# K's low part on 128 rows, the sink by a matmul of ones, and narrower masks in two attention stages

## The chip, the cores and the metric

One core of one Trainium2 chip runs a whole program of two transformer blocks on 1024 tokens. The time is device microseconds of one execution; the kernel before took 3023.18 us as the median of 3 runs (3018.93 to 3025.36). In the names below PE is TensorE (PEld its weight loads), DVE VectorE, ACT ScalarE, POOL GpSimd, SP the engine that issues most DMAs.

## The reference

Only two functions of it are touched by the change. In the first block, sliding-window attention with a sink, 8 heads of 64 over 2 heads of K and V, in 8 blocks of 128 queries:

```python
def gqa_sink_attend(qb, keys, vals, bias, sink_g):
    s = jnp.einsum('bqkgd,bskd->bkgqs', qb, keys) * (DH_A ** -0.5) + bias
    s_sink = jnp.broadcast_to(sink_g[None, :, :, None, None], (b, KV_A, G_A, q, 1))
    p = jax.nn.softmax(jnp.concatenate([s, s_sink], axis=-1), axis=-1)[..., :-1]
    return jnp.einsum('bkgqs,bskd->bqkgd', p, vals)

# for block i: keys are 256 context tokens and up to 384 tokens around the block,
# valid = abs(tq - ts) <= 128 and 0 <= ts < 1024
```

In the second block, chunk-band attention, 8 heads of 64: each chunk of 64 queries sees its own chunk and the 8 before it, with a bias by distance:

```python
s = jnp.einsum('bqhd,bkhd->bhqk', qc, kc) * scale + bias
s = jnp.where(valid, s, -jnp.inf)
p = jax.nn.softmax(s, axis=-1)
out = jnp.einsum('bhqk,bkhd->bqhd', p, vc)
```

## The kernel before

Precise products are made of fp32r parts: a number is a high part (rounded) and a low part (the rest). A head has only 64 features, so Q's high part lies on 64 partitions and its low part on the other 64, and K's high part stands on both halves. One matmul of 128 rows then gives (Q high + Q low) times K high. A second matmul on 64 rows gives Q high times K low.

**Window stage** (`phase_window`, L457, about 194 to 424 us). For each of the 8 query blocks, `win_scores` is called for two groups of four heads. For a head it takes a scores buffer of two PSUM banks (`big`, two rotate; L41 is the matmul helper `mm`) and writes: the sink's column, by an fp32 matmul of the identity with a column of `sink` (L354 loads it, on all partitions); the mask, by an fp32r matmul of the identity `identr` with 384 columns (256 in blocks 0 and 7), of which the middle 128 are zeros; then the band of 384 (or 256) keys and the 256 context keys, high part on 128 rows, low part on 64 rows. VectorE takes the maximum (L510), ScalarE the exponential with its sum (L512), VectorE scales (L517). `win_pv` of the block before transposes the probabilities (L44), copies them (L532 on ACT, L534 on DVE) and multiplies by V into 64 columns of the array (`t<-PT,Va`, tile 128*64). Between blocks pieces of another product are called in, `mods` (`t<-wmod,ct`, tile 128*32), whose weights SP streams from DRAM. The constants are prepared at the end of `phase_win` by GpSimd (L353 to L356); GpSimd's next work is the low part of h (L62).

The lines of `win_scores` that matter:

```python
self.mm(ps[:, 768:769], self.ident, sink[:, h:h + 1], True, True)
self.mm(band, identr, mask[:, mo:mo + bw], True, False)
self.mm(band, q, ks[:, g, kb], False, False)
self.mm(ctx, q, ks[:, g, 0:256], True, False)
self.mm(band, q[r], kl[r, g, kb], False, True)
self.mm(ctx, q[r], kl[r, g, 0:256], False, True)
```

`kl` stands on both halves of the partitions already (`put_k`, L399).

**Band stage** (`phase2_mix`, about 1921 to 2085 us). For 4 pairs of heads, 8 query blocks and the 2 heads of a pair, `band_scores` writes the bias by two matmuls with the reversal `Jr` (high `bh` and low `bl`), K's high part `bks` on 128 rows for the far keys (up to 384) and the near ones (up to 256), in the blocks with five key tiles a far mask `mfr` of 256 columns by the identity, and K's low part `bkl` on 64 rows. Maximum (L1550), exponential (L1552), reciprocal and scaling follow, and `band_pv` transposes (L44), copies (L1572) and multiplies by V (tile 128*64). `band_pair` (L1499) makes the parts of a pair: of the low part (L1515) only the 64 partitions that are used, on VectorE for the first two pairs and GpSimd for the others. Some matmuls of the gated branch lie between.

The order on each engine is not written out here: the framework's planner orders the instructions by its own estimates, and may put matmuls of one head behind those of other work.

Of the kernel before, what the change touches and what calls it, by code (L numbers as in the profile page):

```python
# [6 lines left out]
F32 = mybir.dt.float32  # L7
F32R = mybir.dt.float32r
# [25 lines left out]
class Build:  # L34
# [11 lines left out]
    def warm(self, src, n):  # L46
        """keeps the tensor engine's clock up while the first operands of a phase are made"""
        ps = self.pa()
        for _ in range(n):
            self.mm(ps, src[:, :128], src[:, :512], True, True)  # L50
# [13 lines left out]
    def rsqrt(self, ss, scale, eps=EPS, way="act"):  # L64
        """1 / sqrt(ss * scale + eps) for a small tile"""
# [8 lines left out]
    def rsqrt_bits(self, v, eng):  # L74
        """1 / sqrt(v) by Newton's steps from the exponent's half"""
# [56 lines left out]
    def mod_slab(self, pool, s, ps, bufs):  # L132
        """rows 32g (and 32g + 1: ctx) of ps = silu(c) @ w_mod[:, s * 2048 + g * 512 ...]; yields between loads"""
# [24 lines left out]
    def mod_cols(self):  # L158
        """slab 0 as columns: shift, scale of the first norm"""
# [10 lines left out]
    def norm1(self, xp):  # L170
        """x, ctx -> h^T (hi, lo), two tiles of tokens between yields"""
# [74 lines left out]
    def load_w(self, pool, src, n, ks=8, kb=2, tag="w", rawbufs=3, bufs=5, rk=None):  # L246
        """DRAM [ks*128, n] -> list over k of (hi [128, n], lo [128, n])"""
# [14 lines left out]
    def acc3(self, ps, L, R, k, last):  # L262
        """ps += (Lhi+Llo)^T (Rhi+Rlo) without lo*lo"""
        self.mm(ps, L[0], R[0], k == 0, False)
        self.mm(ps, L[0], R[1], False, False)
        self.mm(ps, L[1], R[0], False, last)

    def phase_win(self):
# [15 lines left out]
        mask = vap.tile([128, 384], F32R, name="mask")  # L284
        sink = vap.tile([128, 8], F32, name="sink")
        self.win_consts = identr, mask, sink
# [5 lines left out]
        with self.pool("t0") as st:  # L292
            mraw = st.tile([128, 384], F32, name="mraw")
# [59 lines left out]
            nc.gpsimd.dma_start(mraw, I["maskA"])  # L353
            nc.gpsimd.dma_start(sink, I["sink"].to_broadcast([128, 8]))  # L354
            nc.gpsimd.tensor_copy(identr, self.ident)
            nc.gpsimd.tensor_copy(mask, mraw)  # L356

# [4 lines left out]
        # ka  # L362
# [13 lines left out]
        # cq  # L376
# [22 lines left out]
    def put_k(self, s, x):  # L399
        """rotated keys [128 (two heads), s] -> hi and lo, each on both halves of the partitions"""  # L400
# [9 lines left out]
    def put_q(self, m, s, x):  # L410
        """rotated queries of heads 2m, 2m + 1 -> hi on one half of the partitions, lo on the other"""
# [7 lines left out]
    def gemm_fm(self, ps, w, c0, act, half_outer=False):  # L419
        """ps [128, 1024] = W[:, c0:c0+128]^T act"""  # L420
# [36 lines left out]
    def phase_window(self, mods):  # L457
        nc, tc, I = self.nc, self.tc, self.I
        with self.pool("wa", "right") as wa:
            qs, ks, kl = self.qs, self.ks, self.kl  # L460
            identr, mask, sink = self.win_consts
            pend = None
            for b in range(8):
                u = self.win_block(wa, b)
                self.win_scores(wa, u, 0, qs, ks, kl, identr, mask, sink)
                if pend:
                    self.win_pv(wa, pend)
                self.win_scores(wa, u, 1, qs, ks, kl, identr, mask, sink)
# [21 lines left out]
    def win_scores(self, wa, u, g, qs, ks, kl, identr, mask, sink):  # L490
# [5 lines left out]
        mo = 0 if b else 128  # L496
        P = []
        for h in range(g * 4, g * 4 + 4):
            r = slice((h % 2) * 64, (h % 2) * 64 + 64)
# [4 lines left out]
            self.mm(ps[:, 768:769], self.ident, sink[:, h:h + 1], True, True)  # L504
            self.mm(band, identr, mask[:, mo:mo + bw], True, False)
            self.mm(band, q, ks[:, g, kb], False, False)
            self.mm(ctx, q, ks[:, g, 0:256], True, False)
            self.mm(band, q[r], kl[r, g, kb], False, True)
            self.mm(ctx, q[r], kl[r, g, 0:256], False, True)
            nc.vector.reduce_max(nm[:, h:h + 1], ps[:, c0:769], axis=AX.X, negate=True)  # L510
            p = wa.tile([128, 642], F32, name="P", bufs=12)
            nc.scalar.activation(p[:, :W + 1], ps[:, c0:769], AF.Exp, bias=nm[:, h:h + 1], accum_out=sm[:, h:h + 1])  # L512
# [93 lines left out]
    def mla_init_k(self, s, w):  # L606
        """the rows of K that all pairs share: rotated keys, the maximum's -1 and zeros between"""
# [43 lines left out]
    def mla_row_max(self, s):  # L651
        """rows of Q: the largest score of every query, from the leading parts"""
# [25 lines left out]
    def mla_early(self):  # L678
        """the first pair of heads: leading parts and largest scores"""
# [175 lines left out]
    def logits(self, wo, h2, t, wr):  # L855
        """the router's scores of the tokens of the tiles h2, the first of them tile t"""
# [33 lines left out]
    def router_softmax(self, g0, g1):  # L890
        """softmax over the experts for groups g0..g1 of two tiles (tile 2g + i at [:, i, g])"""
# [183 lines left out]
    def norm2_tile(self, xp, x, nf, nm, t):  # L1075
        """h^T of a tile of tokens: the final norm of block 1 and the first of block 2 at once"""
# [233 lines left out]
    def gdn_local(self, gp, c):  # L1310
        """k^T, q^T, P^T and U of a chunk, kept in DRAM, with U's diagonal blocks of 32 apart"""
# [30 lines left out]
    def gdn_invert(self, gp):  # L1342
        """(I - U)^-1 of all 128 diagonal blocks of 32, one to a partition, by back substitution"""
# [17 lines left out]
    def gdn_solve(self, gp, c):  # L1361
        """R = (I - U)^-1 of a chunk from its diagonal blocks; yields between stages"""
# [111 lines left out]
    def band_prep(self, bp):  # L1474
# [15 lines left out]
        m = bp.tile([128, 256], F32, name="mfar")  # L1490
        nc.vector.memset(m, 0.0)
        nc.vector.memset(m[64:128, 0:64], -1e30)
        self.mfar = bp.tile([128, 256], F32R, name="mfr")
        nc.vector.tensor_copy(self.mfar, m)

    def band_pair(self, bp, m):
# [7 lines left out]
        for e in range(2):  # L1504
# [10 lines left out]
            eng.tensor_sub(kl[r, e], T[1, e][r], ks[r, e].bitcast(F32))  # L1515
# [5 lines left out]
    def band_scores(self, bp, m, b, pre):  # L1521
# [9 lines left out]
        for e in range(2):  # L1531
            r = slice(e * 64, e * 64 + 64)
# [10 lines left out]
            if nk == 5:  # L1543
                self.mm(ps[:, c0:c0 + 256], self.idr, self.mfar, False, False)
            if far:
                self.mm(pf, q[r], kl[r, e, kf], False, True)
            self.mm(pn, q[r], kl[r, e, kn], False, True)
# [69 lines left out]
    def branch_a(self):  # L1617
        """the gated branch a of the first 256 features, while the bands leave room on the tensor engine"""
# [247 lines left out]
def prepare(inputs):  # L1866
# [6 lines left out]
    A = {}  # L1873
# [35 lines left out]
    z = np.zeros((128, 128), f32)  # L1909
# [56 lines left out]
```

## Time and profile before

| | us |
|---|---|
| median of 3 runs | 3023.18 |
| span of the profiled execution | 3023.2 |
| window stage, first block's third head to the end | 224 to 424 |
| band stage | 1921 to 2085 |

| engine | busy us | share of the span |
|---|---|---|
| TensorE matmul | 2843.3 | 94% |
| TensorE weight load | 2196.4 | 73% |
| VectorE | 1785.1 | 59% |
| ScalarE | 1132.4 | 37% |
| GpSimd | 643.4 | 21% |

The busy time of TensorE is the union of matmuls whose recorded durations overlap in a stream. For the price of one matmul one reads the distance between the starts of neighbours. The granted clock is given as a share: 1.00 is 2.4 GHz, 0.50 is 1.2 GHz.

### The profile page before, as it was taken

The numbers are of one execution on the slowest core, as the hardware profiler recorded it, in microseconds if no ns is written. First come the engines' busy times: TensorE is split into PE (matmuls) and PEld (weight loads), VectorE is DVE, ScalarE is ACT, GpSimd is POOL, SyncE is SP. The second block draws the span as 40 slices with busy tenths as digits, with TensorE's granted clock in tenths as the row PEclk, the third lists the DMA queues.
The fourth block names the chain that finished last, engine by engine and source line by source line (L and its number), as shares of the span: only waits on it lengthen the run. The fifth ranks groups of instructions, "written<-read, shape, count | busy, mean of one in ns | idle before, by whom it ended". The sixth has DMA issues, their size and how long they took to land. (4 is left out here: it accounts for less than half of the span.)

```text
span 3023.2 us, 36522 instructions
## 1 busy us (share of the span) xinstructions
PE 2843.3 (94%) x14196; PEld 2196.4 (73%) x14196; DVE 1785.1 (59%) x2675; ACT 1132.4 (37%) x1756; POOL 643.4 (21%) x622
## 2 busy tenths in 40 slices
PE   6999999999994999789999899999999999999997
PEld 3885556445673777578889788777898888888886
DVE  3654457888567999766436333375655445445445
ACT  4443445334423676553321223454133222222223
POOL 1000013333433888522121332130000000000000
PEclk8998999999996999999999999999999999999999
DMA  6123200000437999822453545212522111111111
GB/s 217 41 69 105 91 29 8 1 1 22 130 128 253 353 372 371 259 64 84 143 183 113 192 140 147 83 37 74 177 85 84 49 52 53 42 49 49 42 35 56
DMA packets 179965, 338.81 MB, mean 112 GB/s; under 512 B 17545, under 2 KB 104457, under 8 KB 177489
## 3 DMA queue, kind: packets, MB, share of 16 engines
q1 hardware_dynamic: 161408, 270.13, 26.9%
q0 software_dynamic: 18384, 66.35, 6.9%
q8 instruction: 112, 1.84, 0.3%
q14 instruction: 61, 0.49, 0.0%
HBM read 282.95 MB, written 53.49 MB: 111 GB/s over the span
## 5 line engine op out<-in xcount | busy, mean ns | idle before, releaser
L62 DVE TENSOR_TENSOR mlo<-mraw,mhi 128x2048 fp32r<-128x2048 f32 x63 | 220.1, 3520 | 9.6 <-ACT mhi L59 9.5
L41 PE MATMUL big<-hhi,wuhi 128*128 128x512 f32 x672 | 214.8, 396 | 0.0
L41 PE MATMUL big<-hhi,wulo 128*128 128x512 f32 x672 | 213.3, 396 | 0.0
L41 PE MATMUL big<-hlo,wuhi 128*128 128x512 f32 x672 | 213.1, 396 | 0.0
L41 PE MATMUL big<-hhi,whi 128*128 128x512 f32 x656 | 210.5, 399 | 0.0
L41 PE MATMUL big<-hlo,whi 128*128 128x512 f32 x656 | 208.5, 396 | 0.0
L41 PE MATMUL big<-hhi,wlo 128*128 128x512 f32 x656 | 207.5, 395 | 0.0
L59 ACT CAST mhi<-mraw 128x2048 fp32r<-128x2048 f32 x96 | 181.5, 1913 | 55.9 <-PE big L41 30.3
L62 POOL TENSOR_TENSOR mlo<-mraw,mhi 128x2048 fp32r<-128x2048 f32 x33 | 164.9, 5004 | 74.1 <-ACT mhi L59 73.7
L1769 DVE TENSOR_TENSOR xs<-xs,t 128x512 f32<-128x512 f32 x176 | 118.0, 686 | 83.3 <-PE t L41 83.2
L1728 DVE SCALAR_TENSOR_TENSOR cacc<-big,cols,cacc 128x1023 f32<-128x1023 f32 (+2 forms) x90 | 113.1, 1257 | 82.6 <-ACT cacc L1724 81.0
L1786 POOL TENSOR_TENSOR wuraw<-wuraw,nf 128x1024 f32<-128x1024 f32 x2 | 5.8, 2900 | 733.1 <-ACT rst L100 729.0
L62 DVE TENSOR_TENSOR wlo<-wraw,whi 128x512 fp32r<-128x512 f32 (+5 forms) x124 | 78.6, 644 | 124.9 <-ACT whi L59 124.3
L765 ACT ACTIVATE P<-t 128x512 f32<-128x512 f32 x160 | 94.6, 597 | 145.5 <-PE t L41 135.0
L41 PEld LDWEIGHTS big<-hhi,wulo 128*128 128x128 f32 x672 | 126.6, 188 | 30.8
L41 PEld LDWEIGHTS big<-hlo,wuhi 128*128 128x128 f32 x672 | 126.6, 188 | 30.8
L41 PEld LDWEIGHTS big<-hhi,wuhi 128*128 128x128 f32 x672 | 126.5, 188 | 30.7
L41 PEld LDWEIGHTS big<-hlo,whi 128*128 128x128 f32 x656 | 122.8, 189 | 26.3
L41 PEld LDWEIGHTS big<-hhi,wlo 128*128 128x128 f32 x656 | 122.8, 188 | 26.1
L41 PE MATMUL t<-wdhi,ah 128*128 128x512 f32 x352 | 137.4, 390 | 1.4 <-ACT ah L59 1.1
L41 PEld LDWEIGHTS big<-hhi,whi 128*128 128x128 f32 x656 | 121.0, 189 | 23.5
L41 PE MATMUL t<-wdlo,ah 128*128 128x512 f32 x352 | 137.2, 390 | 0.0
(596 smaller groups left out, 6939.4 us busy)
## 6 DMA issues: line engine op xcount, KB each, us to landing
mraw<-in_w_gate SPq DMA_DIRECT2D x32, 1024.0 KB, 12.0
mraw<-in_w_up SPq DMA_DIRECT2D x32, 1024.0 KB, 12.5
mraw<-in_w_down SPq DMA_DIRECT2D x32, 1024.0 KB, 10.4
wmod<-in_w_mod SPq DMA_DIRECT2D x48, 512.0 KB, 4.6
wuraw<-in_w_up SPq DMA_DIRECT2D x42, 512.0 KB, 4.0
wraw<-in_w2a SPq DMA_DIRECT2D x72, 256.0 KB, 3.1
wdraw<-in_w_down SPq DMA_DIRECT2D x22, 512.0 KB, 3.2
gxd<-gx POOLq DMA_DIRECT2D x8, 1024.0 KB, 4.7
```

Source lines behind the costliest of these rows:

```text
L41: self.nc.tensor.matmul(out, lhsT, rhs, start=start, stop=stop)
L59: nc.scalar.copy(hi, src)
L62: (nc.vector if lo_eng == "dve" else nc.gpsimd).tensor_sub(lo, src, hi.bitcast(F32))
L765: nc.scalar.activation(P, ps, AF.Exp, scale=self.sc_mla)
L1728: nc.vector.scalar_tensor_tensor(t[:, b:c + w], ps[:, b - tap:c + w - tap], self.col("conv_f", (2 - tap) * 44 + m), t[:, b:c + w], op0=ALU ...
L1769: nc.vector.tensor_add(xs[:, t, cs], xs[:, t, cs], ps)
L1786: nc.gpsimd.tensor_mul(y, y, nf)
```

## The change

In the window stage K's low part is multiplied with all 128 rows of Q, high and low, so that Q low times K low is now in the scores too. The sink's column is made by an fp32r matmul of a matrix of ones with two columns per head: the first has the sink's high part on partition 0 and its low part on partition 32, the second has -1e30. The maximum and the exponential take one column more. The mask matmul is replaced by up to two of 128 columns, for the two blocks of keys that are partly masked, and comes behind the products. The order of a head's matmuls is now band high, band low, masks, context high, context low, sink. In the band stage the low part is made and used on 128 partitions, and the far mask has 64 columns in place of 256. Comments are removed.

```diff
-        mask = vap.tile([128, 384], F32R, name="mask")
-        sink = vap.tile([128, 8], F32, name="sink")
+        mask = vap.tile([128, 2, 128], F32R, name="mask")
+        ones = vap.tile([128, 128], F32R, name="onesr")
+        sink = vap.tile([128, 8, 2], F32R, name="sink")
...
-            nc.gpsimd.dma_start(mraw, I["maskA"])
-            nc.gpsimd.dma_start(sink, I["sink"].to_broadcast([128, 8]))
+            nc.gpsimd.dma_start(mraw, I["maskA"].rearrange("p (a b) -> p a b", a=2))
+            nc.gpsimd.memset(sraw, 0.0)
+            nc.gpsimd.memset(sraw[0:1, :, 1:2], -1e30)
+            for p in (0, 32):
+                nc.gpsimd.dma_start(sraw[p:p + 1, :, 0:1], I["sink"].rearrange("a (h o) -> a h o", o=1))
             nc.gpsimd.tensor_copy(identr, self.ident)
             nc.gpsimd.tensor_copy(mask, mraw)
+            nc.gpsimd.memset(ones.bitcast(F32), 1.0)
+            nc.gpsimd.tensor_copy(sink, sraw)
+            nc.gpsimd.tensor_sub(sink[32:33], sraw[32:33], sink[32:33].bitcast(F32))
...
-            self.mm(ps[:, 768:769], self.ident, sink[:, h:h + 1], True, True)
-            self.mm(band, identr, mask[:, mo:mo + bw], True, False)
-            self.mm(band, q, ks[:, g, kb], False, False)
+            self.mm(band, q, ks[:, g, kb], True, False)
+            self.mm(band, q, kl[:, g, kb], False, False)
+            if b:
+                self.mm(ps[:, c0:c0 + 128], identr, mask[:, 0], False, b == 7)
+            if b < 7:
+                self.mm(ps[:, 384:512], identr, mask[:, 1], False, True)
             self.mm(ctx, q, ks[:, g, 0:256], True, False)
-            self.mm(band, q[r], kl[r, g, kb], False, True)
-            self.mm(ctx, q[r], kl[r, g, 0:256], False, True)
-            nc.vector.reduce_max(nm[:, h:h + 1], ps[:, c0:769], axis=AX.X, negate=True)
+            self.mm(ctx, q, kl[:, g, 0:256], False, True)
+            self.mm(ps[:, 768:770], ones, sink[:, h], True, True)
+            nc.vector.reduce_max(nm[:, h:h + 1], ps[:, c0:770], axis=AX.X, negate=True)
             p = wa.tile([128, 642], F32, name="P", bufs=12)
-            nc.scalar.activation(p[:, :W + 1], ps[:, c0:769], AF.Exp, bias=nm[:, h:h + 1], accum_out=sm[:, h:h + 1])
+            nc.scalar.activation(p[:, :W + 2], ps[:, c0:770], AF.Exp, bias=nm[:, h:h + 1], accum_out=sm[:, h:h + 1])
...
-        m = bp.tile([128, 256], F32, name="mfar")
+        m = bp.tile([128, 64], F32, name="mfar")
...
-            eng.tensor_sub(kl[r, e], T[1, e][r], ks[r, e].bitcast(F32))
+            eng.tensor_sub(kl[:, e], T[1, e], ks[:, e].bitcast(F32))
...
-                self.mm(ps[:, c0:c0 + 256], self.idr, self.mfar, False, False)
+                self.mm(ps[:, c0:c0 + 64], self.idr, self.mfar, False, False)
             if far:
-                self.mm(pf, q[r], kl[r, e, kf], False, True)
-            self.mm(pn, q[r], kl[r, e, kn], False, True)
+                self.mm(pf, q, kl[:, e, kf], False, True)
+            self.mm(pn, q, kl[:, e, kn], False, True)
```

## Rows read from the trace of the kernel before

**Rows 1.** The page: span; busy us, share and instructions of the first engines.

```profile
span 3023.2 us, 36522 instructions
PE 2843.3 (94%) x14196; PEld 2196.4 (73%) x14196; DVE 1785.1 (59%) x2675; ACT 1132.4 (37%) x1756; POOL 643.4 (21%) x622
```

**Rows 2.** Busy time by stretches: length, us busy (instructions) per engine, granted clock, DMA share.

```profile
217.70:224.50 6.80, 5.29 (x37) 3.16 (x35) 0.52 (x2) 4.96 (x9) 0.00 (x0) 0.50 0.84 284
227.90:251.80 23.90, 23.90 (x83) 13.64 (x82) 10.61 (x20) 5.14 (x13) 0.00 (x0) 0.50 0.31 94
251.80:406.00 154.20, 154.20 (x896) 86.29 (x894) 76.16 (x129) 65.48 (x142) 2.59 (x5) 1.00 0.25 79
...
1921.00:1940.00 19.00, 17.41 (x74) 13.17 (x73) 9.24 (x25) 10.98 (x25) 0.53 (x1) 0.64 0.43 139
...
1960.00:1980.00 20.00, 16.49 (x117) 12.71 (x115) 17.52 (x29) 8.57 (x28) 15.27 (x9) 0.83 0.50 132
1980.00:2000.00 20.00, 19.90 (x151) 14.71 (x150) 12.42 (x28) 11.76 (x29) 0.00 (x0) 1.00 0.00 1
```

**Rows 3.** Waits, 194 to 425 us: who waited for whom, total, times, longest.

```profile
DVE nm L510 <- PE big L41: 120.2, 41, 16.4
```

**Rows 4.** Timeline of one head and the reduction before it: start, duration, instruction.

```profile
323.15 0.83 DVE L510 TENSOR_REDUCE nm<-big 128x1 f32<-128x641 f32 x1 [7.81 <-PE big L41]
...
324.01 0.80 ACT L512 ACTIVATE P<-big,nm 128x641 f32<-128x641 f32 x1 [1.25 <-DVE nm L510]
...
326.00 0.38 PE L41 MATMUL big<-sink,ident 128*128 128x1 f32 x2
...
326.24 0.42 PE L41 MATMUL big<-mask,identr 128*128 128x384 f32 x1
...
326.50 0.45 PE L41 MATMUL big<-ks,qs 128*128 128x384 f32 x2
...
326.67 0.28 PE L41 MATMUL big<-ks,qs 128*128 128x256 f32 x1
...
326.88 0.56 PE L41 MATMUL big<-kl,qs 64*128 64x384 f32 x2
327.37 0.38 PE L41 MATMUL big<-sink,ident 128*128 128x1 f32 x2
```

**Rows 5.** Timeline of the band stage, matmuls of two blocks.

```profile
1942.00 0.38 PE L41 MATMUL big<-bh,Jr 128*128 128x256 f32 x1
...
1942.22 0.28 PE L41 MATMUL big<-bl,Jr 128*128 128x256 f32 x1
...
1942.34 0.46 PE L41 MATMUL big<-bks,bqs 128*128 128x384 f32 x2
...
1942.64 0.28 PE L41 MATMUL big<-mfr,idr 128*128 128x256 f32 x1
...
2031.28 0.44 PE L41 MATMUL big<-bkl,bqs 64*128 64x384 f32 x1
2031.65 0.88 PE L41 MATMUL t<-bPT,vb 128*64 128x128 f32 x12
```

**Rows 6.** Timeline: 128-column fp32r matmuls behind one another, at the band stage's start.

```profile
1921.38 0.22 PE L41 MATMUL big<-bh,Jr 128*128 128x128 f32 x1
1921.44 0.27 PE L41 MATMUL big<-bl,Jr 128*128 128x128 f32 x1
1921.55 0.28 PE L41 MATMUL big<-bks,bqs 128*128 128x128 f32 x1
```

**Rows 7.** Timeline: a low-part run of the window stage and what follows it.

```profile
259.52 0.56 PE L41 MATMUL big<-kl,qs 64*128 64x384 f32 x2
260.01 1.07 PE L41 MATMUL t<-PT,Va 128*64 128x512 f32 x2
```

**Rows 8.** Timeline of GpSimd: its first work after the constants, with the idle time before it.

```profile
43.93 0.74 POOL L62 TENSOR_TENSOR clo<-t,chi 128x256 fp32r<-128x256 f32 x1 [34.74 <-DVE chi L61]
```

**Rows 9.** The instructions of line 1515: count, duration in ns (min/median/max), first and last start.

```profile
L1515 DVE TENSOR_TENSOR bkl<-bqk,bks x4: 1216/1219/1223, 1858.0 to 1880.1; 64x1024 fp32r<-64x1024 f32 x4
L1515 POOL TENSOR_TENSOR bkl<-bqk,bks x4: 2358/2478/3318, 1961.4 to 2014.3; 64x1024 fp32r<-64x1024 f32 x4
```

More of the change, by code (lines that the diff above doesn't have):

```diff
@@ L283, in phase_win @@
         identr = vap.tile([128, 128], F32R, name="identr")
-        mask = vap.tile([128, 384], F32R, name="mask")
-        sink = vap.tile([128, 8], F32, name="sink")
-        self.win_consts = identr, mask, sink
+        mask = vap.tile([128, 2, 128], F32R, name="mask")
+        ones = vap.tile([128, 128], F32R, name="onesr")
+        sink = vap.tile([128, 8, 2], F32R, name="sink")
+        self.win_consts = identr, mask, ones, sink
         def hL(t):
@@ L292, in phase_win @@
         with self.pool("t0") as st:
-            mraw = st.tile([128, 384], F32, name="mraw")
+            mraw = st.tile([128, 2, 128], F32, name="mraw")
+            sraw = st.tile([128, 8, 2], F32, name="sraw")
             krc = st.tile([128, 8, 32], F32, name="krc")
@@ L460, in phase_window @@
             qs, ks, kl = self.qs, self.ks, self.kl
-            identr, mask, sink = self.win_consts
+            identr, mask, ones, sink = self.win_consts
             pend = None
@@ L464, in phase_window @@
                 u = self.win_block(wa, b)
-                self.win_scores(wa, u, 0, qs, ks, kl, identr, mask, sink)
+                self.win_scores(wa, u, 0, qs, ks, kl, identr, mask, ones, sink)
                 if pend:
                     self.win_pv(wa, pend)
-                self.win_scores(wa, u, 1, qs, ks, kl, identr, mask, sink)
+                self.win_scores(wa, u, 1, qs, ks, kl, identr, mask, ones, sink)
                 for _ in range(4):
@@ L488, in win_block, with win_scores @@
                     sm=sm.tile([128, 8], F32, name="mmx4"))
-    def win_scores(self, wa, u, g, qs, ks, kl, identr, mask, sink):
+    def win_scores(self, wa, u, g, qs, ks, kl, identr, mask, ones, sink):
         nc = self.nc
@@ L495, in win_scores @@
         c0 = 512 - bw
-        mo = 0 if b else 128
         P = []
         for h in range(g * 4, g * 4 + 4):
-            r = slice((h % 2) * 64, (h % 2) * 64 + 64)
             ps = self.big()
@@ L1489, in band_prep @@
         nc.vector.tensor_copy(self.idr, self.ident)
-        m = bp.tile([128, 256], F32, name="mfar")
+        m = bp.tile([128, 64], F32, name="mfar")
         nc.vector.memset(m, 0.0)
-        nc.vector.memset(m[64:128, 0:64], -1e30)
-        self.mfar = bp.tile([128, 256], F32R, name="mfr")
+        nc.vector.memset(m[64:128], -1e30)
+        self.mfar = bp.tile([128, 64], F32R, name="mfr")
         nc.vector.tensor_copy(self.mfar, m)
@@ L1531, in band_scores @@
         for e in range(2):
-            r = slice(e * 64, e * 64 + 64)
             ps = self.big()
@@ L1908, in prepare @@
     r = np.arange(128)
-    z = np.zeros((128, 128), f32)
     neg = f32(-1e30)
-    A["maskA"] = np.concatenate([np.where(r[None, :] >= r[:, None], f32(0), neg), z,
+    A["maskA"] = np.concatenate([np.where(r[None, :] >= r[:, None], f32(0), neg),
                                  np.where(r[None, :] <= r[:, None], f32(0), neg)], 1).astype(f32)
```

## The prediction, made before the changed kernel was run

> **What bounds the kernel now.** I read the page's totals first: TensorE is busy for 94% of a span of 3023.2 us [rows 1]. The span equals the median of the timed runs (3023.18 us) to within rounding, so sums from this execution need no conversion. An average over so many stages says little about the two that are changed, so I read those next, by stretches. In the window stage TensorE is busy for all 154.20 us from 251.8 to 406, at granted clock 1.00 (the 2.4 GHz level), and for all 23.90 us from 227.9 to 251.8 at 0.50 (1.2 GHz); VectorE and ScalarE are under half busy [rows 2]. The waits agree: VectorE's reductions stood 120.2 us waiting for TensorE's score matmuls [rows 3]. The band stage is mixed: 19.90 of 20 us from 1980 to 2000, but 17.41 of 19 at its start and 16.49 of 20 from 1960 to 1980, where VectorE has 17.52 [rows 2]. So in the window stage a TensorE nanosecond is worth nearly a nanosecond, in the band stage somewhat less.
>
> Busy time doesn't tell what a matmul costs in a stream: recorded durations overlap. What counts is the distance from one start to the next, so I read two short stretches matmul by matmul. The reader should look only at the start column there.
>
> **What a head of the window costs [rows 4].** From one head's first matmul to the next head's is 327.37 - 326.00 = 1.37 us. In it: 0.50 for the fp32 sink (which leaves two records) and the mask; 0.17 for 384 columns of K's high part (326.50 to 326.67); 0.21 from there to the first low-part matmul; 0.49 for the two low-part matmuls, which have the same 384 and 256 columns. A full-height 256-column matmul is followed after 0.12 us (1942.22 to 1942.34), and a full-height 384 + 256 pair takes 0.30 (1942.34 to 1942.64) [rows 5]. The 64-row run therefore pays 0.21 - 0.12 = 0.09 on entry and 0.49 - 0.29 = 0.20 inside and on leaving. The 0.20 splits into about 0.11 and 0.09: in the band stage a lone 384-column low-part matmul takes 0.37 until the next start (2031.28 to 2031.65), again 0.20 over 0.17 [rows 5]. I read 0.09 as the array changing from 128 rows to 64, 0.11 as the first weight load that could not be fetched ahead, 0.09 as changing back. The same sign shows when leaving a 64-column tile: the first Jr matmul after P times V takes 0.22 to the next start (1942.00 to 1942.22), and the one behind it, equally wide, 0.12 [rows 5].
>
> The Trainium skill has a rule for this, in TensorEngine Tiling (Array Packing), Key Properties: a change of tiling mode drains the engine. The trace agrees as to the two 0.09 us steps; the rule says nothing of the 0.11 us load inside the run, and if only the drains went away the gain below would be smaller by about 12 us (0.11 for each of some 140 runs, four fifths of it). The same page (When to Use Tiling) advises row tiling for a contraction of 64, which is the opposite of this change; here no two 64-row matmuls run side by side, since what follows a low-part matmul starts only 0.37 us after it.
>
> **The change, window stage.** *Low part on 128 rows.* Everything is then full height: 0.17 + 0.12 for the pair, and 0.09 + 0.11 + 0.09 = 0.29 us less per head. *Sink.* With the mask at the full-height pace (0.17), the old sink costs 0.50 - 0.17 = 0.33. The new one is a full-height fp32r matmul of 2 columns, a shape that the trace doesn't have. The nearest rows are 128-column fp32r matmuls one after another: 0.06 and 0.11 us [rows 6], the first just behind a long matmul. I take 0.11, the pace of a weight load that has nothing long to hide behind, and keep 0.06 to 0.17 (a 384-column one, which 2 columns shouldn't exceed) as bounds. *Masks.* One matmul of 384 columns (0.17) becomes two of 128 at 0.11: 0.05 dearer in blocks 1 to 6; in blocks 0 and 7 one of 256 (0.12) becomes one of 128. *Sum for a head:* 0.17 + 0.17 + 0.11 + 0.11 + 0.12 + 0.12 + 0.11 = 0.91, against 1.37, so 0.46 less; 48 heads give 22.1 us. In blocks 0 and 7 the band has 256 columns: before 1.37 - 3 x 0.05 = 1.22, after 4 x 0.12 + 2 x 0.11 = 0.70, so 0.52 less, 16 heads give 8.3. About 7 heads run at half clock, where the 0.46 counts twice: 3.2 more. Some 20 of the 70 low-part runs are followed by a tile of 64 or 32 columns, as at 260.01 [rows 7], and the change back stays as a change forward: 20 x 0.09 = 1.8 less. Sum: 31.8 us.
>
> How much arrives? A head's scores buffer (two rotate) comes free after a reduction of 0.83 and an exponential of 0.80: reduced from 323.15, free at 324.81, needed again at 326.00, so 1.2 us of slack [rows 4]. A gain of 0.46 per head fits into it mostly, but three heads in a row would leave only 0.91 us for some 1.7. Block 0 has no P times V to lie between, and the last block has little. I take off 4 us, worked out as some ten heads of those two blocks that keep 0.1 of their 0.5 us: **28 us** from the window stage.
>
> **The change, band stage.** 64 scores (4 pairs x 8 blocks x 2 heads) each lose a run's 0.29: 18.6 us. Some 22 entries and exits touch a 64-column tile and stay, as at 2031.65 [rows 5]: 2.0 less. About 20 runs are followed by the Jr matmuls, whose first load was exposed (0.22 against 0.12): 2.0 more. The 7 runs at half clock at the start add 2.0. The far mask falls from 256 columns (0.12) to 64 (at the load's 0.11, 0.06 at best): 32 x 0.01 = 0.3, at best 1.9. Sum: 20.9 us. Of the 69 runs some 28 lie in stretches where TensorE has gaps (1921 to 1940, 1960 to 1980, 2000 to 2020); there I count half, elsewhere 85%: 20.9 x (28 x 0.5 + 41 x 0.85) / 69 = 14.8, so **15 us**.
>
> **Edits with no price.** The set-up on GpSimd (two memsets of the sink, one more small DMA issue, ones, copy, subtraction) lies between 9.2 and 43.9 us, where GpSimd has nothing: 34.74 us idle before its next work, the split of h at 43.93 [rows 8]. If the added pieces took as long as all of GpSimd's work until 9.2, the queue would end at 18; without the cover that split would be 9 us late. In the band's preparation the subtraction for the low part writes 128 partitions in place of 64, for the same 1024 columns: eight instructions, 1219 ns each on VectorE and 2478 on GpSimd [rows 9]. I take them as unchanged, since an engine works on partitions side by side; were they doubled, it would be 4 x 1.2 and 4 x 2.5 us, well ahead of their use. The subtraction waits for the same copy as before. No DMA is moved past another. The reduction and the exponential each get one column more (1 ns or so), on engines with slack.
>
> **The rivals.**
> *Next bound takes half.* The scores' buffers and in-order VectorE and ScalarE eat the gain: PV copies stand between exponentials in ScalarE's queue. For it: the slack of 1.2 us is of the size of the gain over three heads. Against: 120.2 us of waiting the other way [rows 3]. Half of 43: **3001**. 0.14.
> *Short matmuls are not bound by the weight load.* At 0.06 rather than 0.11, masks and sink save 48 x 2 x 0.05 + 16 x 0.05 + 64 x 0.05 = 8.8, nearly 8 after losses: **2972**. Against it: the second short one in a row took 0.11 [rows 6]. 0.06. The Trainium skill gives even less for such a matmul by itself (TensorE: Matmul & The Clock Gate, Back-to-back issue gap: 134 cycles for 128 columns, about 60 for up to 64), without counting a weight load.
> *The clock rises sooner.* From 227.9 to 251.8 TensorE was full of short and 64-row matmuls and still at 0.50. With fewer changes of mode the level may come back before block 1: half of 23.9 us is 12 more, so **2968**. 0.14.
> *The clock falls: the case on the other side.* It fell to 0.50 at 217.7, when TensorE was busy 5.29 of 6.80 us [rows 2]. If a faster TensorE waits for VectorE and ScalarE in small gaps through the window stage and stays at 0.50 there, the 154.2 us less 24 saved would take up to 130 more: about **3110**. It decides once the lower level lasts some 85 us longer than today (each such microsecond costs half, against 43 gained). For it: a full TensorE at 0.50 in rows 2. Against: the denser mix from 251.8 held 1.00 for 154 us. 0.04.
> *It doesn't do what it says:* 128 rows bring the same gaps, because they belong to the low part's operands and not to its height. Only the sink gains, some 12 us: **3011**. Against: the 64-column tile shows the same exposed load. 0.04; a further 0.02 that nothing is measurable, about 3022.
>
> **How the numbers follow.** 3023 - 28 - 15 = **2980 us**, chance 0.56 with its own range 2970 to 2992. The range that should hold 8 in 10 reaches to 2962 (clock rises sooner and short matmuls cheaper in part) and to 3002 (half arrives, or the masks cost 0.17 each, which is 48 x 2 x 0.06 = 6 us). What is left out: 3011, 3022 and 3110, and the far ends. A measurement of this kernel can tell about 0.2% (6 us) from no change. Faster by more than that: 0.93. Within: 0.03. Slower: 0.04.
>
> **What would show it.** In the changed trace: low-part matmuls with 128 rows, starting 0.17 and 0.12 us apart from their neighbours; a head's seven matmuls in 0.91 us; the sink and the masks at 0.11 (or 0.06); the window stage from its first full head (224) to its end (424) shorter by some 28 us; the band stage (1921 to 2085) shorter by some 15; all stages between merely shifted. Wrong, if gaps before a head's first matmul (released by the exponential) add up to over 10 us, if the granted clock differs by over 20 us in either stage, or if other stages change by more than a few microseconds because the order of the work on an engine changed.

## The result, and the profile after

The changed kernel takes **2990.01 us** (median; 2988.78 to 2993.83) where the kernel before took 3022.99 in the same comparison: a ratio of **0.9889, 95% interval 0.9871 to 0.9908**, or 33 us less (28 to 39). The forecast was 43 less. The profiled execution's span went from 3023.2 to 2987.0 us, and the sums below are made against these two spans.

First the page of the kernel after, which answers to [rows 1]: span, then busy us, share and instructions of each engine.

```profile
span 2987.0 us, 36505 instructions
PE 2798.1 (94%) x14180; PEld 2181.9 (73%) x14180; DVE 1787.8 (60%) x2675; ACT 1132.3 (38%) x1756; POOL 642.1 (21%) x628
```

TensorE is busy 45.2 us less, its share is the same 94%, and no other engine moved by more than 3 us. TensorE's weight loads, which run beside its matmuls, are busy 14.5 us less. That says that the time went out of TensorE's stream, and not in which stage.

To find the stages I read, for a tile's matmuls, the first and the last start in each kernel. The view gives durations in ns (min/median/max), then first and last start in us. P times V of the window stage (t<-PT,Va) and of the band stage (t<-bPT,vb), kernel before:

```profile
L41 PE MATMUL t<-PT,Va x152: 592/629/1113, 241.4 to 436.2; 128*64 128x512 f32 x152
L41 PE MATMUL t<-bPT,vb x480: 272/273/473, 1929.2 to 2090.9; 128*64 128x128 f32 x160
```

and the kernel after:

```profile
L41 PE MATMUL t<-PT,Va x152: 592/604/644, 233.9 to 415.4; 128*64 128x512 f32 x152
L41 PE MATMUL t<-bPT,vb x480: 272/273/476, 1910.2 to 2055.6; 128*64 128x128 f32 x160
```

The last P times V of the window moved from 436.2 to 415.4, so 20.8 us are won by the end of that stage (2.3 of them were there at its start: the first low-part matmul starts at 194.6 before and at 192.3 after). Between the stages 1.8 are lost again (1929.2 to 1910.2 is 19.0). At the end of the band stage it is 35.3 (2090.9 to 2055.6), so the band gave 16.3. The band gave what was forecast. **The window gave some 19 where 28 were forecast.**

Next the clock, as in [rows 2]: stretches of the kernel after, with length, busy us (instructions) of TensorE, weight load, VectorE, ScalarE and GpSimd, granted clock, DMA share and GB/s.

```profile
224.90:228.30 3.40, 3.40 (x19) 2.42 (x21) 3.26 (x8) 1.21 (x4) 0.00 (x0) 0.50 0.87 280
228.30:404.00 175.70, 171.27 (x1038) 101.34 (x1031) 89.96 (x156) 79.54 (x173) 2.99 (x6) 1.00 0.26 80
```

The 23.90 us at 0.50 that the kernel before had at 227.9 to 251.8 are down to 3.40. The 6.80 us at 0.50 ahead of them, from 217.70 [rows 2], have become 3.4, from 214.6, so over the whole stage it is 30.7 before and 6.8 after. A rival of the prediction happened: the clock rose sooner. That by itself should be worth 10 to 12 us (half of the difference). So the window gave 19 *with* 10 or so from the clock, and far less than the forecast without it; the experiments are about where that went. In the band stage the stretches at 0.50 add up to 20.4 us before (from 1924.4 and 1965.3) and 10.2 after, so up to 5 of its 16.3 us may be the clock's too; e2 below bears on that.

A head of the kernel after, matmul by matmul (start, duration, instruction), against [rows 4]:

```profile
302.06 0.42 PE L41 MATMUL big<-ks,qs 128*128 128x384 f32 x1
302.31 0.34 PE L41 MATMUL big<-kl,qs 128*128 128x384 f32 x1
302.49 0.34 PE L41 MATMUL big<-mask,identr 128*128 128x128 f32 x2
302.66 0.33 PE L41 MATMUL big<-ks,qs 128*128 128x256 f32 x1
302.83 0.28 PE L41 MATMUL big<-kl,qs 128*128 128x256 f32 x1
302.94 0.17 PE L41 MATMUL big<-sink,onesr 128*128 128x2 f32 x1
302.97 0.42 PE L41 MATMUL big<-ks,qs 128*128 128x384 f32 x1
```

From 302.06 to 302.97 is 0.91 us, just what the prediction's sum for a head gave. So a head that stands undisturbed in the stream has its price, and the loss must lie elsewhere, or in heads that do not stand so. I added up the distances from each start to the next in the window stage, worked out from the starts in the timeline (224 to 424.5 us before, 221 to 404 after, with 62 heads in each). In the last two columns what ran at 0.50 counts half, which takes the clock out by estimate:

| us from start to start | before | after | before, clock taken out | after, clock taken out |
|---|---|---|---|---|
| scores, masks, sink | 90.9 | 65.3 | 84.0 | 64.4 |
| transposes | 39.5 | 34.1 | 38.1 | 34.1 |
| P times V | 49.1 | 59.3 | 48.1 | 59.3 |
| other, mostly `mods` | 21.0 | 24.1 | 18.1 | 23.3 |
| all | 200.4 | 182.9 | 188.3 | 181.2 |

Of the 17.5 us some 10 are the clock's. The scores gave 19.6, where the prediction's sum without its term for the clock has 28.6. **P times V, which the change doesn't touch, cost 11 us more**, and the other matmuls 5 more (2.1 of them waits for the weights of `mods`).

The groups by line show it too (tile, shape and count | busy us, mean ns | idle time before them and its releaser), TensorE's P times V in the window stage, kernel before:

```profile
L41 PE MATMUL t<-PT,Va 128*64 128x512 f32 x152 | 59.3, 624 | 2.7 <-ACT PT L532 1.4 <-DVE PT L534 1.3
```

and after:

```profile
L41 PE MATMUL t<-PT,Va 128*64 128x512 f32 x152 | 69.7, 617 | 4.3 <-ACT PT L541 2.9 <-DVE ri L524 0.9 <-DVE PT L543 0.4
```

That is 10.4 us more busy time at the same count and a mean duration no longer than before: they overlap less. Why is seen at one pair in the timeline of the kernel after (weight loads are PEld):

```profile
272.83 1.06 ACT L541 COPY PT<-t 128x512 f32<-128x512 f32 x2
273.46 0.19 PEld L41 LDWEIGHTS t<-PT,Va 128*64 128x64 f32 x2 [0.48 <-ACT PT L541]
273.46 1.56 PE L41 MATMUL t<-PT,Va 128*64 128x512 f32 x4 [0.34 <-ACT PT L541]
273.94 0.19 PEld L41 LDWEIGHTS t<-PT,Va 128*64 128x64 f32 x2 [0.30 <-ACT PT L541]
274.95 0.39 PE L41 MATMUL big<-ks,qs 128*128 128x256 f32 x1
```

A P times V has 64 output columns of the array; the two head groups of a key tile use the two halves. The copies to SBUF that feed them run one after the other on ScalarE (272.83, 1.06 us for two). The second group's weight load waits for the second copy and comes at 273.94, 0.48 us behind the first. The pair then holds TensorE from 273.46 to 274.95, 1.49 us; a pair that starts together takes 1.01 (below). Of the stretch's 68 P times V (each leaves two records), 30 run alone in the kernel after, 1 pair runs together and in 18 pairs the second is late; before, the counts were 26, 16 and 5 (worked out from the starts). The waits of the weight load agree. The first line is the kernel before, the others the kernel after (who waited for whom, total, times, longest):

```profile
PEld t L41 <- ACT PT L532: 4.6, 13, 0.7
PEld t L41 <- ACT PT L541: 11.6, 31, 0.6
PEld big L41 <- ACT P L521: 5.6, 10, 1.5
DVE nm L519 <- PE big L41: 96.7, 33, 16.1
```

The third line is the wait for which the prediction took off 4 us, a free score buffer: it was 7.5 us in 10 waits before, so nothing was added there. The last answers to [rows 3]: VectorE still waits for TensorE.

### The profile page after: what moved, and what is told of

Its sections match the earlier page's. It is cut to its first block, busy times and chain, and to the rows that moved or that the text cites. A ratio compares the mean times of both kernels' runs of the same rounds, so it can differ in the third digit from the quotient of the medians.

```text
span 2987.0 us, 36505 instructions
## 1 busy us (share of the span) xinstructions
PE 2798.1 (94%) x14180; PEld 2181.9 (73%) x14180; DVE 1787.8 (60%) x2675; ACT 1132.3 (38%) x1756; POOL 642.1 (21%) x628
## 5 line engine op out<-in xcount | busy, mean ns | idle before, releaser
L41 PEld LDWEIGHTS big<-hhi,wulo 128*128 128x128 f32 x672 | 126.6, 188 | 30.7
L41 PEld LDWEIGHTS big<-hhi,wuhi 128*128 128x128 f32 x672 | 126.5, 188 | 30.7
```

The costliest lines, as they stand in the source:

```text
L41: self.nc.tensor.matmul(out, lhsT, rhs, start=start, stop=stop)
```

## The experiments

Each was timed beside the kernel before on its chip; where two experiments are compared, it is by their ratios to it.

**One part at a time.** e1 is the kernel before with the window's edits only, e2 with the band's only. Their diffs are halves of the change:

```diff
# e1: window
-            self.mm(band, q[r], kl[r, g, kb], False, True)
+            self.mm(band, q, kl[:, g, kb], False, False)
...
# e2: band
-            self.mm(pn, q[r], kl[r, e, kn], False, True)
+            self.mm(pn, q, kl[:, e, kn], False, True)
...
```

> The window stage's edits alone (low part on 128 rows, sink by ones, narrower masks); the band stage as before. If the two stages' gains simply add, as the traces of before and after suggest (the window stage is 19 us shorter, the band stage 18): 3004 us, 3000 to 3008. If the band stage's gain was needed for the window's, or the reverse, it would lie outside.

> The band stage's edits alone. By addition 3005 us, 3002 to 3009, with the window stage as before, cold from 228 to 252 us. If it gave under 8 us, the 18 us seen between the two traces would come from somewhere else.

Measured: e1 0.9949 (0.9931 to 0.9968), 15 us less; e2 0.9943 (0.9920 to 0.9966), 17 us less. e1 lies just outside its range (3008.8 us), e2 within (3008.19). The product of the ratios, 0.9892, is the whole change's 0.9889: within these intervals the parts add. First and last starts, e1's window:

```profile
L41 PE MATMUL t<-PT,Va x152: 592/604/644, 235.3 to 416.9; 128*64 128x512 f32 x152
```

and e2's band:

```profile
L41 PE MATMUL t<-bPT,vb x480: 272/273/477, 1932.3 to 2078.6; 128*64 128x128 f32 x160
```

e1's window ends 19.3 us earlier than before; e2's band is 146.3 us from first to last, against 161.7 before and 145.4 after. It has 17.1 us at 0.50 in that stage, 3.3 fewer than before, so the clock can be no more than 2 of its 15.4 us. The miss is in the window alone.

**The window's low part back on 64 rows.** All else as after.

```diff
-            self.mm(band, q, kl[:, g, kb], False, False)
+            self.mm(band, q[r], kl[r, g, kb], False, False)
...
-            self.mm(ctx, q, kl[:, g, 0:256], False, True)
+            self.mm(ctx, q[r], kl[r, g, 0:256], False, True)
```

> The changed kernel with the window's low part back on 64 rows, all else changed. Theory of the mode's price (0.09 on entry, 0.11 exposed load, 0.09 on leaving, 128 runs now, since the band's and the context's low parts stand apart): 15 to 35 us slower than the changed kernel, 3005 to 3025. Rival, the gaps belong to the low part's operands: no difference, 2990. Rival, the window stage is bound by the copies for P times V now: under 8 us slower, as slower scores would leave the copies more time.

Measured: 3058.08 us, 1.0112 (1.0090 to 1.0134): 68 us above the kernel after, and slower than before. The sign is right and the size missed. All of it lies in the window stage, whose last P times V starts at 483.9. Its timeline, a late pair of P times V and the next head:

```profile
300.81 1.56 PE L41 MATMUL t<-PT,Va 128*64 128x512 f32 x4
302.30 0.38 PE L41 MATMUL big<-ks,qs 128*128 128x256 f32 x1
...
303.05 0.42 PE L41 MATMUL big<-ks,qs 128*128 128x384 f32 x1
303.41 0.44 PE L41 MATMUL big<-kl,qs 64*128 64x384 f32 x1
303.78 0.44 PE L41 MATMUL big<-mask,identr 128*128 128x128 f32 x2
304.05 0.33 PE L41 MATMUL big<-ks,qs 128*128 128x256 f32 x1
304.31 0.38 PE L41 MATMUL big<-kl,qs 64*128 64x256 f32 x1
304.63 0.27 PE L41 MATMUL big<-sink,onesr 128*128 128x2 f32 x1
```

In the order of the changed code the two low parts of a head do not stand together: 128 runs of 64 rows in the stage in place of 71 before, as the expectation had it. At the prediction's 0.29 us that is 37 us. This head takes 1.78 us against 0.91, more than two runs at that price; over the stage, with the clock taken out as above, the scores take 103.2 us against 64.4, or 0.31 for each of the 124 runs in the stretch. What I had not counted is the clock: three long stretches at half speed (columns as in the stretches above; the second row is the one ahead of the second fall).

```profile
227.00:261.00 34.00, 34.00 (x99) 16.93 (x98) 11.18 (x20) 8.21 (x20) 0.00 (x0) 0.50 0.26 81
330.00:339.00 9.00, 9.00 (x47) 4.99 (x47) 3.17 (x4) 3.75 (x9) 2.15 (x5) 1.00 0.21 62
339.00:353.00 14.00, 14.00 (x47) 7.05 (x47) 4.99 (x9) 4.17 (x10) 0.29 (x1) 0.51 0.24 76
407.00:421.00 14.00, 14.00 (x49) 7.23 (x47) 4.99 (x9) 4.51 (x10) 0.00 (x0) 0.52 0.20 64
```

With two short ones it is 68 us at 0.50 in the stretch where the kernel after has 3.4. Half of the difference is 32, and the scores' 39 + 32 = 71, less some 2 on the other matmuls, are the 68. TensorE had no gap in any of the three, and none in the 9 us ahead of 339: here the clock fell in the midst of a full stream, one with 64-row runs in it.

e3 shows one thing more. The planner gave its matmuls the order of the kernel after on TensorE, one by one through the stage (898 records beside those of `mods`, worked out from the starts); they are only slower. If P times V came too early because the scores in front of it had got shorter, the pairs should be whole again here. They are not: 30 run alone, 2 pairs together and 17 with the second late, against 30, 1 and 18; the pair above holds 1.49 us (300.81 to 302.30), as in the kernel after. It is the order that the planner wrote for the changed code that brings the lateness, and not the speed at which TensorE goes through it.

**The sink in fp32 again**, at its new place behind the low part.

```diff
-            self.mm(ps[:, 768:770], ones, sink[:, h], True, True)
+            self.mm(ps[:, 768:769], ones, sink[:, h:h + 1], True, True)
```

> The changed kernel with the sink's column by the fp32 matmul of the identity again, at its new place. By the traces 64 x (0.33 - 0.09) = 15 us of TensorE: 3005 if all of it shows. If the window stage is bound by the copies for P times V: under 8 us, below 2998.

Measured: 2997.06 us, 0.9914 (0.9891 to 0.9936). That is 7 us above the kernel after, but the two intervals overlap, so the total alone does not settle it. It lies below the bound of 2998 that stood for copies as the limit, but as the sink turns out cheaper than that expectation had it (below), this says nothing of the copies; the same edit is repeated below on a quieter base, where a row gives its price.

**TensorE's order written out by hand.** If P times V loses because its copies are late, an order that gives the copies time should win the loss back, and more in the kernel after than in the one before. In e5 the window stage of the kernel after fixes TensorE's order: the seven matmuls of a head together, then the transposes of one key tile for both groups, then P times V of the key tile *before*, both groups one behind the other. P has 13 buffers in place of 12, and the pieces of `mods` have other places; these were not tried apart. e6 is the same order with the matmuls of the kernel before.

```diff
+            with tc.manual_schedule(engines={mybir.EngineType.PE}):
...
+            if last:
+                for g in range(2):
+                    self.mm(po[g * 64:(g + 1) * 64], self.Va[:, kts[i - 1], g * 64:(g + 1) * 64], last[g],
+                            i == 1, i == len(kts))
+            last = new
...
```

> The changed kernel with TensorE's order in the window stage written out by hand: a head's seven matmuls together, then the transposes of a key tile for both groups, then P times V of the tile before for both groups one right behind the other. Theory: the gain of the change was lost since P times V of the two groups (two halves of the array's columns) ran side by side less often, 59 us instead of 49 in the stage; with all 36 pairs together it takes some 37 us and the kernel 2965 to 2975. Rival, ScalarE's copies are the bound whatever the order: 2985 to 2995.

> The kernel before (64-row low part, fp32 sink, wide masks) with the same order written out in the window stage. If a head costs 1.37 us against 0.91 and the order keeps everything else alike, the window stage is 25 to 30 us longer than in the changed kernel in that order, and the band stage 17 us: 43 to 47 us slower than that one, 3010 to 3020. If copies bind in that order, the distance is only the band's 17 and a little.

Measured: e5 **2954.08 us, 0.9766** (0.9749 to 0.9784), faster than both kernels; e6 3004.99 us, 0.9937 (0.9924 to 0.9950). By the ratios, the order alone is worth 0.0123 or 37 us to the kernel after and 0.0063 or 19 to the one before, and in the same order the change is worth 0.0171 or 52 us and not 33. Both come out faster than expected (2965 to 2975, and 3010 to 3020). P times V takes 36.0 us in e5, as was forecast; with the clock taken out it gives 24 us of the window's 33, the other matmuls 8 and the scores 6, and the transposes take 4 back. The groups of P times V in e5 and e6:

```profile
L41 PE MATMUL t<-PT,Va 128*64 128x512 f32 x140 | 38.4, 628 | 0.0
```

```profile
L41 PE MATMUL t<-PT,Va 128*64 128x512 f32 x140 | 38.7, 631 | 0.0
```

(The stretch ends a little earlier here, so 140 of the 152 records are counted.) The idle time before them is gone. A head of e6 runs from its sink to the transposes behind it, 300.65 to 302.03 or 1.38 us:

```profile
300.65 0.38 PE L41 MATMUL big<-sink,ident 128*128 128x1 f32 x2
...
302.03 1.09 PE L44 MATMUL t<-ident,P 128*128 128x128 f32 x8
```

In e5's timeline a pair costs 283.58 to 284.58, one microsecond:

```profile
283.58 1.08 PE L41 MATMUL t<-PT,Va 128*64 128x512 f32 x4
284.58 0.44 PE L41 MATMUL big<-ks,qs 128*128 128x384 f32 x1
```

In e5 all 35 pairs of the stretch run together, 34 at 1.009 us for two and the last, at half clock, at 1.69; in e6, with the slower scores, it is the same. So fast and slow scores both have whole pairs in this order, and both have late ones in the planner's (after and e3). A lone one in the kernel before took 253.82 to 254.82, 1.00 us:

```profile
253.82 1.07 PE L41 MATMUL t<-PT,Va 128*64 128x512 f32 x2
254.82 0.66 PE L44 MATMUL t<-ident,P 128*128 128x128 f32 x4
```

So the second group of a pair costs nothing if it starts with the first, and a full microsecond if it stands alone. The Trainium skill has the rule in TensorEngine Tiling (Array Packing), Key Properties: different tiles can load weights and multiply in parallel. These rows agree; how late the second may come, and what it then costs, only the rows tell (0.48 us late, 1.49 for the pair).

**Half of the copies on VectorE**, the order left to the planner.

```diff
-                if (i + g) % 3:
+                if (i + g) % 2:
```

> The changed kernel with half instead of a third of the transposed probabilities copied by VectorE. If P times V comes late because ScalarE's copies do: 4 to 8 us faster than the changed kernel, 2982 to 2986. If VectorE, which also takes the maxima, is as late: no change or slower, 2990 to 2996.

> The changed kernel in the written-out order with half of the copies on VectorE. In that order no pair of P times V waits for a copy, so the copies' engine should no longer matter: 2951 to 2957, against the 9 us that the same edit gave in the planner's order. If it gives 6 us or more again, the copies were late for ScalarE's sake and not only for the order's.

Measured: e8 2981.32 us, 0.9855 (0.9840 to 0.9870), 10 us less than the kernel after, whose interval begins at 0.9871; the last P times V starts at 406.8 in place of 415.4. e11 is the same edit in e5's order: 2953.93 us, 0.9761 (0.9743 to 0.9779), no difference from e5. By the two ratios' intervals the 10 us are 3 to 17; the end of the window stage moved by 8.6. Where the copies are on time, spreading them more evenly over two engines buys nothing; where they are late, it buys some 10 us. That is what lateness of the copies predicts. It mends little of the pairs, though: in e8, 23 P times V run alone, 5 pairs together and 18 with the second late, and from start to start they take 52.9 us, where it was 59.3 after, 49.1 before and 36.0 in e5. Faster copies win back a part; what makes the rest is which matmul stands next in the queue.

**The clock by itself.** e7 is the kernel before with 24 idle matmuls of 512 columns in the first block, whose results nobody reads.

```diff
+                if b == 0:
+                    self.warm_win(qs)
...
+    def warm_win(self, qs):
+        ps = self.pa(0, 2)
+        for _ in range(12):
+            self.mm(ps, qs[:, 0, :128], qs[:, 0, :512], True, True)
```

> The kernel before with 24 idle 512-column full-height matmuls among the first block's heads (some 5 us of added work, results unused). Theory: the stretch at 1.2 GHz from 228 to 252 us goes, which gives 10 to 12 us back: 5 to 7 us faster than before, 3016 to 3018. If the clock falls there for another reason, the stretch stays and the kernel is 5 us slower, 3028.

Measured: 3022.66 us, 0.9989 (0.9978 to 1.0000). By the ratio that is 3 us less than before (0 to 7), where 5 to 7 were expected; the time itself, 5 us above the range, comes from a group of runs in which the kernel before took 3025.34 too. The stretches show the clock doing what was wanted:

```profile
217.80:221.20 3.40, 3.05 (x13) 2.55 (x12) 0.50 (x2) 1.65 (x3) 0.00 (x0) 0.50 1.09 370
221.20:419.30 198.10, 196.15 (x1125) 110.94 (x1124) 95.18 (x164) 85.57 (x187) 2.99 (x6) 1.00 0.27 83
```

and the last P times V of the window starts at 431.1, 5.1 us earlier than before, in spite of the added matmuls, which hold TensorE for some 6 us. So an early clock is worth some 11 us in this stage; half of the 27.3 us that no longer run at 0.50 would be 13.7. The total, 3 us less (0 to 7), does not contradict the 5.1. By the band stage the gain was gone in the profiled execution: its first P times V starts at 1930.3, 1.1 us *later* than before. But that execution, at 3028.62 us, was the longest of e7's twelve, 6 us above their median, and it lost its lead in stages that the edit doesn't touch: the last matmul `t<-tb,J` still starts 3.1 us earlier than before (947.7 before), the last `t<-g,cm` 1.9 later (1338.5 before). One execution cannot tell what an edit is worth at the end of the kernel.

**The 64 rows and the fp32 sink once more, in the fixed order,** where nothing else moves.

> The changed kernel in the written-out order, but with the window's low part on 64 rows and its two matmuls together (64 runs). At 0.29 us a run for entry, exposed load and return: 18.6 us more than the changed kernel in that order (2954), plus up to 10 us if the first blocks stay at 1.2 GHz longer: 2972 to 2984. If the price belonged to the low part's operands and not to its height: 2954.

> The changed kernel in the written-out order, but with the sink by an fp32 matmul of the identity, last in a head. By the step lengths 0.33 against 0.11 at most: 64 x 0.2 = 13 us more, 2964 to 2970. If the two records of the fp32 matmul cost only one load each (0.22 - 0.11): 7 us more, 2961.

The edits are those of e3 and e4, made to e5; in e9 the two low parts of a head stand together, so that there are 64 runs. Measured: e9 2981.96 us, 0.9853 (0.9829 to 0.9876), 26 above e5 by the ratios (0.0087). A head of e9:

```profile
301.77 0.44 PE L41 MATMUL big<-ks,qs 128*128 128x384 f32 x1
...
302.22 0.33 PE L41 MATMUL big<-ks,qs 128*128 128x256 f32 x1
302.48 0.56 PE L41 MATMUL big<-kl,qs 64*128 64x384 f32 x2
302.96 0.27 PE L41 MATMUL big<-sink,onesr 128*128 128x2 f32 x1
```

The low parts start 0.26 after the 256-column matmul, where it is 0.17 in e5, and hold 0.48, against 0.29 for full height: 0.28 in all, close to the prediction's price. 64 x 0.29 = 18.6 us; the clock's part is the stretch

```profile
217.90:248.60 30.70, 29.19 (x132) 19.29 (x131) 13.24 (x24) 13.63 (x27) 0.00 (x0) 0.50 0.56 183
```

at 0.50, against 6.8 us in e5: (30.7 - 6.8) / 2 = 12. Together 30.6. The total gives 26, with some 9 of noise either way; in the profiled executions the window, from its first low-part matmul to its last P times V, takes 218.0 us against e5's 187.5, 30.5 more. The head shown loses more, 1.33 against 0.94 us, since the sink behind the low part is dearer as well (below); against that e5 has 4.6 us of idle time before its score matmuls and transposes, and e9 none. e10: 2960.24 us, 0.9783 (0.9764 to 0.9801), 6 above e5 and e11, again with intervals that overlap. Its sink and the next start:

```profile
301.87 0.28 PE L41 MATMUL big<-sink,ident 128*128 128x1 f32 x2
302.01 1.07 PE L44 MATMUL t<-ident,P 128*128 128x128 f32 x8
```

and a whole head of e5, of which the sink is the last step:

```profile
301.58 0.44 PE L41 MATMUL big<-ks,qs 128*128 128x384 f32 x1
...
302.49 0.17 PE L41 MATMUL big<-sink,onesr 128*128 128x2 f32 x1
302.52 0.65 PE L44 MATMUL t<-ident,P 128*128 128x128 f32 x4
```

The fp32 sink costs 0.14 us there and the fp32r one 0.03: 0.11 apart, 64 times, is 7 us. Ahead of a tile of 64 or 32 columns it is 0.21 and 0.10, again 0.11 apart. That is the second of the two forecasts. The totals of e4 and e10 agree with it, but could not have told it from nothing.

## Why the prediction was right, and where not

**A head's price: right.** 0.91 forecast, 0.91 measured; in the fixed order a head takes 1.38 in e6 and 0.94 in e5 (301.58 to 302.52), 0.44 less where 0.46 was forecast.

**A 64-row run's 0.29 us: right.** e9 shows it in the rows (0.09 on entry, 0.19 inside and on leaving), and in the window's length with the clock's part beside it. How the 0.19 divides between a load and a change back is the prediction's reading; no run tells them apart. That the gaps came with the low part's operands and not with its height (the rival at 3011) is refuted by e9 and e3.

**The band: right.** 15 forecast; 16.3 between first and last P times V, 17 (10 to 24) by e2, where the clock has little part in it.

**Edits with no price: right.** The subtraction over 128 rows takes 1226 ns on VectorE and 2492 on GpSimd, 1219 and 2478 before [rows 9]; GpSimd is done with the constants at 10.9 us, 32.3 before its next work.

**The split of a head among its edits: wrong, the sum notwithstanding.** The sink was sized at 0.33 old and 0.11 new, 0.22 less. By itself it is 0.11 less (e10). The old figure held 0.10 that belongs to the 64-row run in front of it: in the kernel before the fp32 sink takes 0.24 until the next start behind a low part [rows 4] and 0.14 behind a transpose; in e9, behind a low part, the cheap sink too takes 0.133, and 0.03 in e5 (worked out from the starts). In turn the low part was worth that much more. In the head of the kernel after the first 384-column matmul costs 0.26 and not 0.17 (302.06 to 302.31), the two masks 0.17 and not 0.22 (302.49 to 302.66), the first 256-column matmul 0.17 and not 0.12 (302.66 to 302.83), and the new sink 0.03 and not 0.11 (302.94 to 302.97). It looks as if a short matmul hid behind the long one ahead of it and the next paid for it. Terms that err by 0.05 to 0.1 cancelled, which was luck.

**How much arrives: the step that failed.** I looked for a cover that would run out, named the score buffer with its 1.2 us of slack, and took off 4 us. That wait did not grow. What I put at nothing, without a reason, is the rest of the stage's stream: that P times V and the other matmuls would cost what they cost before, and that the heads would stand as whole as before. The planner wrote another order for the changed code, and in it P times V stands too soon behind its transposes for ScalarE's copies. Of the pairs that ran side by side, 16 became 1: 11 us, paid as busy TensorE, so that neither the page's 94% nor TensorE's idle time shows it. The scores kept back 9 us of their 28.6; in the fixed order they give 23.4 (82.1 in e6 to 58.7 in e5), so part of that is the order too. The last sentence of the prediction names the cause in passing (other stages change "because the order of the work on an engine changed"), but for other stages only, not within this one. That the order decides whether the pairs are whole is shown with fast and slow scores in either order: late in the kernel after and in e3, whole in e5 and e6. That the copies are what the late ones wait for is shown by the waits, e8 (some 10 us) and e11 (none). Why the planner chose that order is not shown.

**The clock: a rival that came true** beside the forecast, not in place of it. It is also one of the prediction's own signs of being wrong: the granted clock differs by 23.9 us in this stage, where 20 was the limit. (The sign before it did not come: the gaps released by the exponential are 5.6 us.) Without its 10 us or so the window would have given 7 to 9, a third of the 28. That the total came within 10 us of the forecast is luck in part: two errors of opposite sign. In the fixed order, where the pairs are whole, the window's first low part to last P times V takes 217.0 us in e6 (195.0 to 412.0) and 187.5 in e5 (191.2 to 378.7): 29.5 less. In that time e6 has 30.7 us at 0.50 and e5 13.7, so some 8 of these are the clock, and the matmuls give about 21 of the 28. I have not traced the rest.

**Left open.** Every kernel here whose window has its low part on 64 rows stayed at 0.50 for 20.5 to 34.1 us in one stretch at the start of the stage (before, e2, e3, e6, e9), but for e7 with its added matmuls; every one with 128 rows (after, e1, e4, e5, e8, e10, e11), for 3.4 to 6.8 at most. That is five kernels against seven without an overlap, and e3 differs from the kernel after in the low part's height alone, with the same order of matmuls. Why the chip does it is not shown.

## What to carry to other kernels

Price a matmul from start to start, and price every change of tile height: here a 64-row run among 128-row matmuls cost 0.29 us and a slow clock on top, so padding the contraction to 128 rows was the faster way. When an engine's work changes and a planner orders it, look at the new order, and at what now stands right behind the work that feeds it; two matmuls on two column halves cost as much as one only if both operands are there, and the loss of that shows as busy time, not as waiting. Here writing the order out by hand gave 37 us, more than the change itself.

## What the runs showed of the hardware that was not expected

- Two fp32 matmuls of 512 columns on the two 64-column halves take 1.01 us together and a lone one 1.00. With the second 0.48 us late the pair takes 1.49.
- An fp32r matmul of 2 columns behind one of 256 columns holds the stream for 0.03 us, and for 0.10 ahead of a tile of 64 or 32 columns. At the same places an fp32 one of one column (two records) holds it for 0.14 and 0.21.
- With TensorE busy for all of 34.0 us, and again for 14.0 and 14.0, the granted clock was 0.50 to 0.52 (1.2 GHz) in e3, amid single 64-row runs; with 128 rows in the same stage it was 1.00 from 228.3 to 404.
- The early return of the clock, brought about by 24 idle matmuls that cost some 6 us, ended the stage 5.1 us earlier; of the whole kernel it was 3 us (0.9989, 0.9978 to 1.0000).
